# The expert stage of a two-model block: low halves on GpSimd during top-k, wide one-hots, and gate groups spread from the end of top-k

## Chip, cores and metric

The kernel runs on 1 core of one Trainium2 chip. The metric is the device time of one execution in microseconds (us); the time before is the median of 3 runs.

## What is computed

The reference is one first block (state-space mixer, sliding-window attention, gates, and an expert mixer) and two further layers, on 256 tokens of 1024 features in float32. The change lies in the expert mixer, which retrieves 16 of 16384 single-neuron experts in each of 8 heads for every token:

```python
q = (xt @ w_query).reshape(t, PEER_HEADS, 2, PEER_KEY_DIM // 2)
s = jnp.einsum('thkd,hknd->thkn', q, sub_keys)
vals, idx = lax.top_k(s, PEER_TOPK)
cand = (vals[:, :, 0, :, None] + vals[:, :, 1, None, :]).reshape(t, PEER_HEADS, 256)
best, pos = lax.top_k(cand, PEER_TOPK)
expert = i1 * N_SUB_KEYS + i2
gate = softmax(best)
a = einsum('cd,ced->ce', xb, u_tab[eb])
w = gb * gelu(a)
out = einsum('ce,ced->cd', w, v_tab[eb])
```

The kernel does not gather. It computes gelu(x u^T) for all 16384 experts, multiplies by a gate matrix that is zero outside the chosen experts, and multiplies by all of v.

## The kernel before

**Weights as a stream.** `Stream` (lines 80 to 146) loads weight pieces of 128 x 1024 float32 (512 KB) through the queue of SyncE into 3 raw buffers. Each piece is split in two float32r parts: ScalarE casts a high part (`whi`, L125), and VectorE or GpSimd subtracts it from the raw piece to give the low part (`wlo`, L127). A piece is split in two halves of 128 x 512 (`CUT = 2`), and a string names the engine of each half: `'vg'` is the first half on VectorE (v), the second on GpSimd (g); a single letter takes both. There are 3 pairs of part buffers, so the split runs at most 3 pieces ahead of TensorE.

**The product with u.** `gemm_t` (L214) takes 128 pieces of `peer_u`. A piece is 8 blocks of 128 features against 256 tokens, and each block is three matmuls (L210 to L212: high x high, high x low, low x high), so 24 matmuls a piece. `evict` applies Gelu on ScalarE into `store[:, piece, tokens]` (L990). After each piece `step()` issues background work.

**Background work.** `Background.step(n)` runs n steps of the generator `topk`, whose instructions count for the scheduler 200 later than where they stand (`LATE`). `STEP` gives 9 steps in 8 pieces. For each of two halves of the tokens, `topk` computes the scores with 16 float32 matmuls of 64 rows (L1063; two passes each in the trace), finds for each of 8 heads the best 16 of 128 on both sides (`top16`, L1049 to L1053, on VectorE), adds the two lists on GpSimd (L1071), finds the best 16 of 256 sums, then looks up the indices in 16-bit operations (L1076 to L1090) and transposes indices and gates (L1101 to L1105).

**Gate groups.** From piece 80 (`FIRST`) on, `quad(q)` handles 4 tokens. `onehots` makes one-hot columns: A and B by comparison (L957, L958), B times the high part of the gate (L959) on VectorE, B times its low part (L960) on GpSimd. Eight matmuls (L972, L973) form the gates of all 16384 experts for the 4 tokens in one of two PSUM banks. VectorE multiplies the pieces already in `store` by them (L977), ScalarE writes the rest as they are (L979), and later pieces are multiplied as they are evicted (L987 on ScalarE, L988 on VectorE). 64 groups are spread to piece 127. All queues are in order: ScalarE runs L979 after L977, and its later casts wait behind it.

**The product with v** follows (`gemm_acc`, L272 to L274): 128 pieces of 12 matmuls of 512 columns, its left side split from `store` (L1015, L1016).

Of the kernel before, what the change touches and what calls it, by code (L numbers as in the profile page):

```python
# [7 lines left out]
F32 = mybir.dt.float32  # L8
# [71 lines left out]
class Stream:  # L80
    """Weights in the order of their use: loads run ahead, each piece is split into
    two float32r parts whose sum is the float32 value, or is used as it is (lo None)."""
# [12 lines left out]
    def _loads(self, most=None):  # L95
        """A slot is free again when its piece is split, or used where it is not split."""
# [82 lines left out]
class Banks:  # L179
    """PSUM tiles of a bank each, in the given banks in turn."""  # L180
# [10 lines left out]
class Once:  # L191
    """A function called once for each argument."""
# [10 lines left out]
class Kernel:  # L203
# [10 lines left out]
    def gemm_t(self, n_sub, kt, xh, xl, evict, m_per=None, pool=None, step=None):  # L214
        """out^T: per piece of the stream m_per blocks of 128 outputs, tokens along the columns."""
# [76 lines left out]
    def tokens(self):  # L292
        """The two parts of 1024 features of all tokens, the tokens along the columns."""
# [13 lines left out]
    def rsqrt(self, w, y, x):  # L307
        """Newton's iteration, from halved exponent bits."""
# [9 lines left out]
    def residual(self, b, i, ps, sums=True, scale=None):  # L318
        """h += product; the sum of its squares over each half of the row, as 1 / 1024 of it."""
# [14 lines left out]
    def transposed_parts(self, src, i, xh, xl, tp, rev=None):  # L334
        """src: [128 tokens, n]; xh + xl = its transpose, in [128, n / 128, tokens of half i]; rev: a permutation of the tokens."""
# [1342 lines left out]
```

## Time and profile before

| what | value |
|---|---|
| runs | 1868.23, 1873.42, 1876.27 us; median 1873.42 |
| profiled execution | span 1866.1 us, 30817 instructions; no other time is given for it, so its span stands for it, 7.3 us under the median |
| product with u | 355.9 to 857.9 us of the span |
| product with v | from 860.9 us |

Times in the profile are counted from the start of the span. The row of an engine gives its busy time; a matmul's duration overlaps that of the next, so TensorE's pace is read from the distances of starts. "PEclk" is the granted clock as a share of full speed. A wait is put down to what ended it.

### The profile page before, as it was taken

What the parts mean: (1) busy time and instruction counts of PE and PEld (TensorE: products, weight loads), DVE (VectorE), ACT (ScalarE), POOL (GpSimd) and SP (SyncE); (2) the same over time, 40 slices, a digit from 0 to 9 for tenths busy, and PEclk for the clock granted to TensorE, in tenths of its full rate; (3) what the DMA queues carried; (4) which work ended last, traced back from release to release, by engine and by line L of the source; (5) the groups of instructions that cost most, each with busy time, mean ns of one, the idle gap of its engine ahead of it and who ended that gap; (6) DMA issues with size and microseconds to landing.
All of it is one profiled execution on the core that took longest, in us unless ns stands there. A gap on an engine that the chain in (4) does not pass through costs nothing.

```text
span 1866.1 us, 30817 instructions
## 1 busy us (share of the span) xinstructions
PE 1747.6 (94%) x10940; PEld 1532.0 (82%) x10940; DVE 1188.4 (64%) x2521; ACT 899.4 (48%) x2087; POOL 871.3 (47%) x692
## 2 busy tenths in 40 slices
PE   7878899998989988889999999989999998999998
PEld 5456697988989988888888888777799877779986
DVE  7789845377792699996555555567765236775522
ACT  4232544434444433334555555555566445556643
POOL 2465338435444566654444444441354454145443
PEclk9888999989999999999999999999999999999999
DMA  7121235535456533334666666553365555335564
GB/s 251 53 84 46 82 122 171 156 106 168 141 154 182 158 113 102 114 102 159 192 194 195 196 195 192 176 177 105 113 190 183 190 177 185 111 105 192 181 196 143
DMA packets 81543, 282.38 MB, mean 151 GB/s; under 512 B 9659, under 2 KB 12524, under 8 KB 81388
## 3 DMA queue, kind: packets, MB, share of 16 engines
q1 hardware_dynamic: 81388, 280.41, 47.6%
q8 instruction: 86, 1.41, 0.3%
q14 instruction: 69, 0.57, 0.1%
HBM read 279.30 MB, written 1.07 MB: 150 GB/s over the span
## 4 chain that ended last, share of the span: by engine, by line
PE 67%; DVE 19%; issue 5%; POOL 4%; ACT 2%; DMA 2%; SPq 0%; DVEq 0%; POOLq 0%; ACTq 0%
PE acc L272 9%; PE acc L274 9%; PE acc L273 9%; PE acc L210 9%; PE acc L212 9%; PE acc L211 9%; DVE wlo L127 4%; POOL wlo L127 2%; DVE store L988 2%; PE acc L242 1%; PE acc L241 1%; PE acc L243 1%; DVE spare L958 1%; PE o L1396 1%; DVE store L977 1%
## 5 line engine op out<-in xcount | busy, mean ns | idle before, releaser
L127 POOL TENSOR_TENSOR wlo<-raw,whi 128x512 fp32r<-128x512 f32 (+1 forms) x486 | 655.4, 1358 | 700.1 <-ACT whi L125 625.3
L125 ACT CAST whi<-raw 128x512 fp32r<-128x512 f32 (+2 forms) x1004 | 581.8, 612 | 428.3 <-PE acc L211 132.5
L127 DVE TENSOR_TENSOR wlo<-raw,whi 128x512 fp32r<-128x512 f32 (+2 forms) x518 | 437.4, 860 | 320.3 <-ACT whi L125 309.7
L212 PE MATMUL acc<-xh,wlo 128*128 128x256 f32 x1824 | 527.9, 290 | 15.8 <-DVE wlo L127 13.1
L210 PE MATMUL acc<-xh,whi 128*128 128x256 f32 x1824 | 532.6, 293 | 3.1 <-ACT whi L125 2.4
L211 PE MATMUL acc<-xl,whi 128*128 128x256 f32 x1824 | 527.1, 289 | 0.4 <-DVE xl L332 0.3
L212 PEld LDWEIGHTS acc<-xh,wlo 128*128 128x128 f32 x1824 | 358.8, 197 | 21.2 <-DVE wlo L127 16.0
L210 PEld LDWEIGHTS acc<-xh,whi 128*128 128x128 f32 x1824 | 360.2, 198 | 10.0 <-issue 3.6
L211 PEld LDWEIGHTS acc<-xl,whi 128*128 128x128 f32 x1824 | 359.7, 197 | 4.5 <-issue 2.6
L272 PE MATMUL acc<-whi,wh 128*128 128x512 f32 x512 | 199.3, 389 | 2.7 <-ACT wh L1015 2.7
L273 PE MATMUL acc<-wlo,wh 128*128 128x512 f32 x512 | 199.3, 389 | 0.0
L274 PE MATMUL acc<-whi,wl 128*128 128x512 f32 x512 | 199.1, 389 | 0.0
L1015 ACT CAST wh<-store 128x256 fp32r<-128x256 f32 x128 | 51.9, 407 | 160.2 <-PE acc L273 159.3
L1016 DVE TENSOR_TENSOR wl<-store,wh 128x256 fp32r<-128x256 f32 x128 | 54.2, 425 | 114.4 <-ACT wh L1015 114.4
L272 PEld LDWEIGHTS acc<-whi,wh 128*128 128x128 f32 x512 | 96.1, 188 | 23.0 <-ACT wh L1015 3.0
L274 PEld LDWEIGHTS acc<-whi,wl 128*128 128x128 f32 x512 | 96.1, 188 | 19.9
L273 PEld LDWEIGHTS acc<-wlo,wh 128*128 128x128 f32 x512 | 96.1, 188 | 19.8
L273 PE MATMUL acc<-wlo,fh 128*128 128x512 f32 x256 | 99.7, 389 | 0.0
L274 PE MATMUL acc<-whi,fl 128*128 128x512 f32 x256 | 99.7, 389 | 0.0
L272 PE MATMUL acc<-whi,fh 128*128 128x512 f32 x256 | 99.6, 389 | 0.0
L960 POOL TENSOR_TENSOR spare<-spare,gl 128x512 f16<-128x512 f16 x64 | 75.8, 1189 | 49.5 <-PE g L973 38.2
L972 PE MATMUL g<-oh 128*128 128x128 f16 x256 | 63.4, 295 | 21.8 <-ACT store L979 20.9
(382 smaller groups left out, 2656.6 us busy)
## 6 DMA issues: line engine op xcount, KB each, us to landing
raw<-in_peer_u_dram SPq DMA_DIRECT2D x128, 512.0 KB, 3.6
raw<-in_peer_v_dram SPq DMA_DIRECT2D x128, 512.0 KB, 3.6
raw<-in_w_ff_dram SPq DMA_DIRECT2D x128, 512.0 KB, 3.9
raw<-in_w_out_dram SPq DMA_DIRECT2D x24, 512.0 KB, 3.7
raw<-in_w_in_g_dram SPq DMA_DIRECT2D x16, 512.0 KB, 3.7
raw<-in_w_in_qkv_dram SPq DMA_DIRECT2D x12, 512.0 KB, 4.7
raw<-in_w_attn_branch_dram SPq DMA_DIRECT2D x8, 512.0 KB, 3.6
raw<-in_peer_w_query_dram SPq DMA_DIRECT2D x8, 512.0 KB, 4.2
```

What stands on the lines that cost most here:

```text
L125: nc.scalar.copy(hi[:, x], src[:, x])
L127: eng.tensor_tensor(out=lo[:, x], in0=src[:, x], in1=hi[:, x].bitcast(F32), op=OP.subtract)
L210: t.matmul(ps, wh, xh, start=first, stop=False)
L211: t.matmul(ps, wh, xl, start=False, stop=False)
L212: t.matmul(ps, wl, xh, start=False, stop=last)
L272: t.matmul(ps[i][n], xh[:, ts], w[0][:, ns], start=first, stop=False)
L273: t.matmul(ps[i][n], xh[:, ts], w[1][:, ns], start=False, stop=False)
L274: t.matmul(ps[i][n], xl[:, ts], w[0][:, ns], start=False, stop=last)
L960: g.tensor_tensor(out=Bl, in0=B, in1=b(ids[3]), op=OP.mult)
L972: te.matmul(ps[:, t], A[:, :, t], Bh[:, :, t], start=True, stop=False)
L1015: s.copy(wh, store[:, c])
L1016: v.tensor_tensor(out=wl, in0=store[:, c], in1=wh.bitcast(F32), op=OP.subtract)
```

## The change

Six things change in the expert stage; comments elsewhere are dropped and line numbers move by 3 or 4 in `topk`.

```diff
-FIRST = 80
-STEP = lambda c: 1 + (c % 8 == 0)
-PU = 'vg vg gv'
-PU1 = 'vg'
-NU1 = 0
+STEP = lambda c: 1 + c % 2
+PU = 'v'
+PU1 = 'g g gv'
+NU1 = 48
+LAST = 126
...
-                self.acc, tp, gp = self.banks(0, 1, 2), self.banks(7, 6), self.banks(3, 4)
+                self.acc, tp, gp = self.banks(0, 1, 2), self.banks(7, 6), self.banks(3, 4, 5)
...
-                    A, Bh, B, Bl = oh[:, 0], oh[:, 1], spare[:, q % 2], spare[:, 2 + q % 2]
-                    v.tensor_tensor(out=A, in0=io4, in1=b(ids[0]), op=OP.is_equal)
-                    v.tensor_tensor(out=B, in0=io4, in1=b(ids[1]), op=OP.is_equal)
-                    v.tensor_tensor(out=Bh, in0=B, in1=b(ids[2]), op=OP.mult)
-                    g.tensor_tensor(out=Bl, in0=B, in1=b(ids[3]), op=OP.mult)
+                    v.tensor_tensor(out=AB, in0=io4.unsqueeze(1).to_broadcast(both), in1=b(ids), op=OP.is_equal)
+                    v.tensor_tensor(out=B, in0=AB[:, 1].unsqueeze(1).to_broadcast(both), in1=b(gts), op=OP.mult)
...
-                    if c >= FIRST - 6:
-                        self.bg.drain()
-                    want = (T // 4 * (c - FIRST)) // (127 - FIRST)
+                    if done["from"] is None:
+                        if not self.bg.q:
+                            done["from"] = c
+                        return
+                    want = (T // 4 * (c - done["from"])) // (LAST - done["from"])
...
+                ps = [tp.tile([128, 4, 128], F32, name="tp", tag="tp") for _ in range(2)]
+                for x in range(4):
+                    h = 4 * hg + x
+                    for k in range(2):
+                        rows = slice(64 * k, 64 * k + 64)
+                        te.matmul(ps[k][:, x], qT[rows, h, ts], sk[rows, h], start=True, stop=True)
                 for k in range(2):
-                    ps = tp.tile([128, 4, 128], F32, name="tp", tag="tp")
-                    rows = slice(64 * k, 64 * k + 64)
-                    for x in range(4):
-                        h = 4 * hg + x
-                        te.matmul(ps[:, x], qT[rows, h, ts], sk[rows, h], start=True, stop=True)
-                    s.copy(sc[:, k, 4 * hg:4 * hg + 4], ps)
+                    s.copy(sc[:, k, 4 * hg:4 * hg + 4], ps[k])
...
-            v.tensor_copy(ids[0][:, ts], ps[:, 0])
-            v.tensor_copy(ids[1][:, ts], ps[:, 1])
+            v.tensor_copy(ids[:, :, ts], ps[:, 0:2])
```

In words: of the first 48 pieces of u, five of six low halves go to GpSimd; of the other 80, all go to VectorE. `topk` gets 3 steps in 2 pieces. Four one-hot operations of 128 x 512 become two of 128 x 1024, all on VectorE. The gate groups start when `topk` has been issued and end at piece 126. They get a third PSUM bank. The score matmuls alternate between the upper and the lower 64 rows, into two banks.

**How the rows move, 1: GpSimd, first heads of top-k** (L1071, now L1075, is the addition of the two lists of one head; `wlo` rows are low halves, and the numbers tell pieces apart). Before, and then after:

```order
L127 TENSOR_TENSOR wlo_3410<-raw_3297,whi_3409 128x512
L1071 TENSOR_TENSOR store_2822<-store_2822 128x256
L127 TENSOR_TENSOR wlo_3449<-raw_3336,whi_3448 128x512
L1071 TENSOR_TENSOR store_2822<-store_2822 128x256
L127 TENSOR_TENSOR wlo_3494<-raw_3376,whi_3493 128x512
L127 TENSOR_TENSOR wlo_3533<-raw_3415,whi_3532 128x512
L1071 TENSOR_TENSOR store_2822<-store_2822 128x256
```

```order
L127 TENSOR_TENSOR wlo_3424<-raw_3306,whi_3423 128x512
L1075 TENSOR_TENSOR store_2822<-store_2822 128x256
L127 TENSOR_TENSOR wlo_3469<-raw_3345,whi_3468 128x512 x2
L1075 TENSOR_TENSOR store_2822<-store_2822 128x256
L127 TENSOR_TENSOR wlo_3508<-raw_3390,whi_3507 128x512 x2
L1075 TENSOR_TENSOR store_2822<-store_2822 128x256
L127 TENSOR_TENSOR wlo_3553<-raw_3429,whi_3552 128x512
L127 TENSOR_TENSOR wlo_3592<-raw_3474,whi_3591 128x512
```

Between the first and the eighth addition stood 10 low halves of 10 pieces; now there are 15 halves of 9 pieces.

**2: VectorE, in the middle of the gate groups** (L977, now L978, multiplies `store` by a group's gates; L957 to L959, now L960 and L961, make one-hots; L988, now L989, multiplies an evicted piece). Before, and then after:

```order
L977 SCALAR_TENSOR_TENSOR store_2822<-g_7635,store_2822 128x104x4
L957 TENSOR_TENSOR oh_7752<-io4_2872,i1_3154 128x512
L958 TENSOR_TENSOR spare_3158<-io4_2872,i2_3155 128x512
L959 TENSOR_TENSOR oh_7752<-spare_3158,gh_3156 128x512
L957 TENSOR_TENSOR oh_7805<-io4_2872,i1_3154 128x512
L988 TENSOR_TENSOR store_2822<-gt_7679,store_2822 128x128
L977 SCALAR_TENSOR_TENSOR store_2822<-g_7688,store_2822 128x105x4
L977 SCALAR_TENSOR_TENSOR store_2822<-g_7704,store_2822 128x105x4
L127 TENSOR_TENSOR wlo_7716<-raw_7530,whi_7715 128x512
```

```order
L978 SCALAR_TENSOR_TENSOR store_2822<-g_7001,store_2822 128x86x4
L127 TENSOR_TENSOR wlo_7013<-raw_6879,whi_7012 128x512
L961 TENSOR_TENSOR spare_3156<-oh_7049,gts_3155 128x1024
L960 TENSOR_TENSOR oh_7188<-io4_2872,ids_3154 128x1024
L127 TENSOR_TENSOR wlo_7064<-raw_6916,whi_7063 128x512
L989 TENSOR_TENSOR store_2822<-gt_7045,store_2822 128x128
L978 SCALAR_TENSOR_TENSOR store_2822<-g_7052,store_2822 128x87x4
```

The period between two gate multiplications now holds both low halves of a piece and one wide operation of each kind. The first L978 stands at 47 pieces.

**3: TensorE, the scores of the first tokens** (L1063, now L1066; the other rows are the product with u). Before, and then after:

```order
L210 MATMUL acc_3417<-xh_2826,whi_3330 128x256
L1063 MATMUL tp_3194<-store_2822 128x128
L211 MATMUL acc_3417<-xl_2827,whi_3330 128x256
L1063 MATMUL tp_3194<-store_2822 128x128
L212 MATMUL acc_3417<-xh_2826,wlo_3331 128x256
L1063 MATMUL tp_3194<-store_2822 128x128
```

```order
L211 MATMUL acc_3392<-xl_2827,whi_3300 128x256
L1066 MATMUL tp_3192<-store_2822 128x128
L212 MATMUL acc_3392<-xh_2826,wlo_3301 128x256
L1066 MATMUL tp_3193<-store_2822 128x128
L1066 MATMUL tp_3192<-store_2822 128x128
L1066 MATMUL tp_3193<-store_2822 128x128
```

Each score matmul stood between two matmuls of the product; now 7 of the first 8 stand in a row, and the two banks alternate. The 32 score matmuls stand in 4 bunches, two per half of the tokens, with one or two matmuls of the product inside each.

## Rows read from the trace of the kernel before

**Rows 1.** The page: busy time, share of the span and instructions of each engine.

```profile
PE 1747.6 (94%) x10940; PEld 1532.0 (82%) x10940; DVE 1188.4 (64%) x2521; ACT 899.4 (48%) x2087; POOL 871.3 (47%) x692
```

**Rows 2.** Stretches: length; busy (instructions) PE, PEld, DVE, ACT, POOL; PEclk, DMA, GB/s.

```profile
373.20:397.40 24.20, 24.20 (x107) 19.26 (x106) 13.09 (x66) 6.58 (x13) 5.17 (x6) 0.72 0.22 70
...
423.40:450.10 26.70, 21.79 (x170) 20.46 (x169) 25.25 (x51) 12.54 (x25) 11.48 (x8) 1.00 0.45 137
...
476.00:501.90 25.90, 25.90 (x157) 21.89 (x156) 20.82 (x78) 9.41 (x19) 10.00 (x9) 0.93 0.33 106
...
530.80:558.80 28.00, 22.85 (x170) 21.88 (x170) 24.41 (x40) 12.95 (x25) 12.66 (x9) 0.94 0.49 154
558.80:628.20 69.40, 69.40 (x581) 69.40 (x581) 20.42 (x28) 33.95 (x72) 31.92 (x25) 1.00 0.60 184
628.20:857.90 229.70, 207.94 (x1666) 202.37 (x1664) 221.85 (x338) 83.03 (x254) 142.85 (x111) 0.97 0.37 112
857.90:860.90 3.00, 0.25 (x3) 0.06 (x1) 1.91 (x3) 1.92 (x5) 1.26 (x1) 1.00 0.81 261
```

**Rows 3.** Timeline of ScalarE, 595 to 612 us: two evictions (start, duration).

```profile
597.17 0.38 ACT L990 ACTIVATE store<-acc 128x256 f32<-128x256 f32 x1
...
600.05 0.38 ACT L990 ACTIVATE store<-acc 128x256 f32<-128x256 f32 x1
```

**Rows 4.** Waits, 628.2 to 857.9 us (total us, times, longest).

```profile
ACT store L979 <- DVE store L977: 124.1, 57, 4.5
...
PE g L972 <- ACT store L979: 20.9, 20, 2.5
```

**Rows 5.** Waits, 373 to 560 us (total us, times, longest).

```profile
POOL store L1071 <- DVE store L1052: 28.8, 12, 7.0
...
PE acc L212 <- DVE wlo L127: 9.8, 8, 2.5
```

**Rows 6.** Timeline of TensorE, 845.9 to 846.6 us: matmuls of one gate group.

```profile
845.61 0.30 PE L973 MATMUL g<-spare,oh 128*128 128x128 f16 x1
...
846.32 0.29 PE L973 MATMUL g<-spare,oh 128*128 128x128 f16 x1
```

**Rows 7.** Timeline of TensorE, 379 to 394 us: score matmuls, two passes each.

```profile
385.78 0.49 PE L1063 MATMUL tp<-store 64*128 64x128 f32 x2
...
386.51 0.48 PE L1063 MATMUL tp<-store 64*128 64x128 f32 x2
...
388.86 0.79 PE L1063 MATMUL tp<-store 64*128 64x128 f32 x2
...
390.09 0.79 PE L1063 MATMUL tp<-store 64*128 64x128 f32 x2
```

**Rows 8.** Line L127, 566 to 628 us (ns min/median/max, first and last start).

```profile
L127 POOL TENSOR_TENSOR wlo<-raw,whi x22: 1291/1292/1301, 566.2 to 627.0; 128x512 fp32r<-128x512 f32 x22
L127 DVE TENSOR_TENSOR wlo<-raw,whi x21: 691/693/1040, 568.2 to 626.1; 128x512 fp32r<-128x512 f32 x21
```

**Rows 9.** Lines L957, L977, L988 (ns min/median/max), 632 to 858 us.

```profile
L957 DVE TENSOR_TENSOR oh<-io,i x60: 407/411/1525, 632.2 to 849.6; 128x512 f16<-128x512 f16 x60
...
L977 DVE SCALAR_TENSOR_TENSOR store<-g,store x64: 481/578/680, 633.4 to 855.5; 128x332 f32<-128x332 f32 x2, 128x344 f32<-128x344 f32 x2, 128x356 f32<-128x356 f32 x2, 128x368 f32<-128x368 f32 x2
...
L988 DVE TENSOR_TENSOR store<-gt,store x46: 160/1131/1454, 636.3 to 854.6; 128x4 f32<-128x4 f32 x1, 128x8 f32<-128x8 f32 x1, 128x16 f32<-128x16 f32 x1, 128x20 f32<-128x20 f32 x1
```

**Rows 10.** VectorE in top-k, 400 to 570 us: groups by shape; line L1089; the page's L1016.

```profile
L1052 DVE MAX8 store<-store 128x8 f32<-128x128 f32 x25 | 6.7, 273 | 0.0
...
L1049 DVE MAX8 store<-store 128x8 f32<-128x256 f32 x14 | 5.9, 422 | 1.1 <-POOL store L1071 0.8
...
L1053 DVE MATCH_VALUE_LOAD store<-store 128x8 f32 x40 | 2.9, 72 | 0.1
...
L1089 DVE TENSOR_TENSOR store<-store x12: 277/686/1772, 436.2 to 551.9; 128x1024 f16<-128x1024 f16 x4, 128x512 f16<-128x512 f16 x4, 128x256 f16<-128x256 f16 x4
...
L1016 DVE TENSOR_TENSOR wl<-store,wh 128x256 fp32r<-128x256 f32 x128 | 54.2, 425 | 114.4 <-ACT wh L1015 114.4
```

More of the change, by code (lines that the diff above doesn't have):

```diff
@@ L944, in peer @@
                 self.gemm_t(8, 8, xh, xl, lambda m, ps: s.copy(qT[:, m], ps))
-                ids = [w.tile([128, T], F16, name=n) for n in ("i1", "i2", "gh", "gl")]
-                self.bg.add(self.topk(w, tp, scratch, qT, sk, iota, ids))
-                done = {"t": 0, "c": 0, "q": 0, "oh": {}}
-                spare = self.const.tile([128, 4, 128, 4], F16, name="spare", tag="gain")
-                def onehots(q):
-                    ts = slice(4 * q, 4 * q + 4)
-                    b = lambda x: x[:, ts].unsqueeze(1).to_broadcast([128, 128, 4])
-                    oh = self.stay.tile([128, 2, 128, 4], F16, name="oh", tag="xr", bufs=XR)
-                    A, Bh, B, Bl = oh[:, 0], oh[:, 1], spare[:, q % 2], spare[:, 2 + q % 2]
-                    v.tensor_tensor(out=A, in0=io4, in1=b(ids[0]), op=OP.is_equal)
-                    v.tensor_tensor(out=B, in0=io4, in1=b(ids[1]), op=OP.is_equal)
-                    v.tensor_tensor(out=Bh, in0=B, in1=b(ids[2]), op=OP.mult)
-                    g.tensor_tensor(out=Bl, in0=B, in1=b(ids[3]), op=OP.mult)
-                    done["oh"][q] = (A, Bh, Bl)
+                ids = w.tile([128, 2, T], F16, name="ids")
+                gts = w.tile([128, 2, T], F16, name="gts")
+                self.bg.add(self.topk(w, tp, scratch, qT, sk, iota, ids, gts))
+                done = {"t": 0, "c": 0, "q": 0, "oh": {}, "from": None}
+                spare = self.const.tile([128, 2, 2, 128, 4], F16, name="spare", tag="gain")
+                both = [128, 2, 128, 4]
+                def onehots(q):
+                    b = lambda x: x[:, :, 4 * q:4 * q + 4].unsqueeze(2).to_broadcast(both)
+                    AB = self.stay.tile(both, F16, name="oh", tag="xr", bufs=XR)
+                    B = spare[:, q % 2]
+                    v.tensor_tensor(out=AB, in0=io4.unsqueeze(1).to_broadcast(both), in1=b(ids), op=OP.is_equal)
+                    v.tensor_tensor(out=B, in0=AB[:, 1].unsqueeze(1).to_broadcast(both), in1=b(gts), op=OP.mult)
+                    done["oh"][q] = AB[:, 0], B[:, 0], B[:, 1]
                 def quad(q):
@@ L1027, in peer, with topk @@
                 self.gemm_acc(range(128), Once(lhs), ps, self.residual)
-    def topk(self, w, tp, scratch, qT, sk, iota, ids):
+    def topk(self, w, tp, scratch, qT, sk, iota, ids, gts):
         nc = self.nc
@@ L1101, in topk @@
                 te.transpose(ps[:, k], e3[:, k], self.ident)
-            v.tensor_copy(ids[0][:, ts], ps[:, 0])
-            v.tensor_copy(ids[1][:, ts], ps[:, 1])
-            v.tensor_scalar(ids[2][:, ts], ps[:, 2], 1024.0, None, op0=OP.mult)
-            v.scalar_tensor_tensor(ids[3][:, ts], ps[:, 2], 1024.0, ids[2][:, ts], op0=OP.mult, op1=OP.subtract)
+            v.tensor_copy(ids[:, :, ts], ps[:, 0:2])
+            v.tensor_scalar(gts[:, 0, ts], ps[:, 2], 1024.0, None, op0=OP.mult)
+            v.scalar_tensor_tensor(gts[:, 1, ts], ps[:, 2], 1024.0, gts[:, 0, ts], op0=OP.mult, op1=OP.subtract)
             yield
```

## The prediction, made before the run

> **What bounds the kernel now.** The page comes first: TensorE is busy 94% of the span and VectorE 64% [rows 1], but a mean hides stages, so the second view is the table of stretches over the product with u. Its pace is set by TensorE alone where nothing else happens: two evictions lie 2.88 us apart [rows 3], and 24 pieces (581 matmuls, 24 a piece) take 69.4 us at full clock [rows 2], 2.89 each. The other stretches are read against this floor, with the pieces counted by dividing the matmuls by 24.
>
> Scores: 3 pieces take 24.2 us where 8.6 would do, and 5 take 25.9 where 14.4 would do; together 27.1 us over the floor, at clocks of 0.72 and 0.93 [rows 2]. Rest of top-k: twice 7 pieces (170 matmuls) take 26.7 and 28.0 us where 20.2 would do, 14.3 us over, with VectorE nearly full [rows 2]. There TensorE's third matmul waits for a low part from VectorE [rows 5]. Gate stage: 48 pieces (1666 matmuls less 512 of the groups) take 229.7 us where 138.2 would do, 91.5 over, and VectorE is busy for 221.9 of it [rows 2]. So three quarters of the time lies at the floor, and the last stretch is VectorE's.
>
> Of the 91.5 us, TensorE's own matmuls take some: starts within a group lie (846.32 - 845.61) / 6 = 0.118 us apart [rows 6], 512 x 0.118 = 60.4. The other 31.1 is waiting. The waits name it: ScalarE stood 124.1 us behind VectorE's L977, and TensorE 20.9 us for ScalarE's L979 to free a bank of the gates [rows 4]. Then comes 3.0 us before the product with v starts [rows 2]. The stage in total is 128 x 2.88 = 368.6, plus 60.4, 27.1, 14.3, 31.1, 3.0 and a remainder of 0.5: 505.0 us. The change leaves the first two terms as they are; only 76 us can be won, all of it in the other terms.
>
> **Gate stage: 31.1 us becomes 3.** The groups now start near piece 46 and end at 126, so 80 pieces carry 64 groups, 0.80 each. TensorE then needs 2.88 + 0.80 x 8 x 0.118 = 3.63 us a piece. VectorE's share: a low half takes 0.69 us while nothing holds it up, two are 1.39 [rows 8]. Blocked operations are much longer: the same comparison of 128 x 512 takes 0.41 us at best and 1.53 at worst, and a multiplication of at most 256 columns has a median of 1.13 although one of 256 columns takes 0.43 elsewhere [rows 9, 10]. GpSimd has no work left in this stage, by the order, so I take the short ends. A wide one-hot operation does not exist before; its nearest row is the 16-bit one of 128 x 1024 in L1089, among whose shapes the median 0.686 is that shape's undisturbed time [rows 10], and twice the comparison, 0.82, bounds it above while nothing blocks it [rows 9]. I take 0.69. L978 works on 47 to 126 pieces times 4 columns: from (680 - 481) ns over 508 - 332 columns [rows 9], 1.13 ns a column, I get 0.50 us at the mean of 86 pieces. L989 is 0.16 to 0.43, 0.29 at the mean. The sum is 1.39 + 0.29 + 0.80 x (2 x 0.69 + 0.50) = 3.18 us a piece under TensorE's 3.63. A piece that carries a group needs 3.56 against 3.82, so it fits even singly, though by little. Near the end L978 is 0.68 and L989 0.43, 3.88 against 3.82, and every fifth piece without a group pays that back. The order supports this: after L978 stands the second low half, whose cast is not behind that group's L980, then both one-hot operations, so VectorE rarely waits. The third bank takes the 20.9 us of bank waits off. What is late next is the eviction behind L980. I leave 3 us; the ends are 0 and the present 31.
>
> The four low-gate multiplications on GpSimd vanish into VectorE, counted above. Loads of weights are the same in number and order on SyncE's queue, and at 3.63 us a piece they come slower than now.
>
> **Scores: 27.1 becomes 15.** All 32 score matmuls stood singly. At full clock one plus the matmul it precedes takes 0.73 us, at half clock 1.23 [rows 7]. Now they stand in 4 bunches. A pair of passes lasts 0.48 to 0.49 us at full clock [rows 7]: 32 x 0.48 = 15.4. Below, alternating halves could run side by side, 7.7; above, nothing changes, 27.1. The clock fell to its lower level (1.2 of 2.4 GHz) in these stretches while TensorE ran scores and product in turn; whether bunches avoid that no row shows. I take 15. The Trainium skill, page "TensorEngine Tiling (Array Packing)", section "Key Properties", says that changing the tiling mode drains the engine and that different tiles can compute in parallel. By that the sum would be the lower end, 7 us better than mine. No row here has such a pair, and I keep the serial price.
>
> **Top-k: 14.3 becomes 18.** A head costs VectorE two searches of 128 columns and one of 256: 2 x (5 x 0.273 + 3 x 0.072) + 5 x 0.42 + 3 x 0.072 = 5.5 us [rows 10]. By the order, 7 heads now pass while 9 pieces are split: 38.5 us plus two low halves, 40, against 25.9 on TensorE. Before, 7 heads took 10 pieces: 38.5 + 6.9 = 45 against 28.8. The deficit is 14 instead of 16 per half of the tokens, and 3 part buffers, 8.6 us, cover some of it. In its favour before, score matmuls of the second four heads filled TensorE's time; they now come earlier. So the heads themselves are about even. The lookups after them are the risk: their 16-bit operations take 0.69 or 1.77 us for the same shape [rows 10], a difference of about one GpSimd subtraction, 1.29 [rows 8], and GpSimd now does 1.67 halves a piece instead of one. I add 4 us: 18, with ends of 6 and, in the rival below, 67.
>
> The rule behind these rows is in the Trainium skill, page "SBUF — State Buffer", section "Who interferes with whom": a VectorE instruction with two SBUF inputs and a GpSimd instruction that reads SBUF block one another. The trace agrees for the lookups (0.69 and 1.77), and by it the first 48 pieces are where this change can lose.
>
> **Start of v: 3.0 becomes 1.5**, since the last groups stand at piece 126 with two pieces behind them; ends 0 and 3.
>
> The sum: 368.6 + 60.4 + 15 + 18 + 3 + 1.5 + 0.5 = 467 against 505, which is 38 us less. I allow 3 us for the first group, which stands right behind the second half's lookups on VectorE: 35 us. The profiled execution would go from 1866.1 to 1831; its span is 7.3 us under the median of the runs, so from the median 1873.4 I predict **1838 us**.
>
> **Rivals.**
> - *Everything fits, and pairs of scores overlap.* Scores 8, top-k 8, nothing for the first group: 20 us better, 1818. For it: no engine is full on the new counts. Against: VectorE is full in top-k in either order.
> - *Half of it.* Gate stage left with 15 of its 31 us, since ScalarE still waits behind L978 once a group and a group's period has only 0.26 us of slack on VectorE: 1850 to 1858.
> - *The wide operations run at one element a cycle, or the range of patterns slows them.* Two low halves of 512 float32 columns cost 1.39 [rows 8], so 1024 columns at that pace cost about 1.3. VectorE needs 1.39 + 0.29 + 0.80 x (2.6 + 0.5) = 4.16 a piece, 0.53 over TensorE, 80 x 0.53 = 42 us of waiting, more than the 31 now: the 39 us in its place eat the gain, and the time is 1874 to 1878, no change. Against: the 16-bit rows of 2 and 4 patterns already run faster than that.
> - *Top-k is throttled by GpSimd.* GpSimd waited for VectorE before 12 additions, 28.8 us in all and 7.0 at worst [rows 5]. It then held half of the low parts; now it holds five of six, and each wait delays the next pieces. If the prefetch covers nothing, 14 intervals cost 5.9 (a head and its share of low halves) less 9 / 7 x 2.88 = 3.7, 2.2 each, 31 us, and the 28 two-input operations of the lookups at 1.29 us of blocking each add 36: 67 instead of 18, which makes it 1887, **slower**. It decides against the change from a top-k loss of 18 + 35 = 53 us.
>
> That the change does not do what it says can be set aside for the order: the rows above show the moves.
>
> **How the numbers follow.** The forecast has a chance of 0.50, everything fits 0.14, half of it 0.15, the wide operations 0.09, GpSimd 0.12. About 0.5% of 1873, 9 us, is what a measurement can tell from no change. Faster by more than that: 0.50 + 0.14 + 0.15 less a small share of the worst of these, 0.77; within it 0.11; slower 0.12. The range runs from 1816, the everything-fits case, to 1868, past the half case; it leaves out most of the last two rivals and a little below.
>
> **What would show it.** In the profile after: GpSimd idle from about piece 48 to the end of u; L127 on VectorE near 0.69 us there, L960 and L961 near 0.69 and L989 under 0.45; no wait of TensorE for L980; steps of 3.6 us a piece with VectorE at some 88%. In top-k: score rows in bunches, and waits of TensorE for a low part from GpSimd instead of VectorE. The prediction is wrong if the gate stage runs above 3.8 us a piece, if wide operations cost over 1 us, or if TensorE loses over 50 us in the first 48 pieces.

## The result, and the profile after

| | before | after |
|---|---|---|
| median of the runs (lowest to highest), us | 1870.83 (1866.82 to 1876.27), 4 runs | 1826.06 (1824.68 to 1826.87), 4 runs |
| profiled execution: span, us | 1866.1 | 1822.9 (its time 1824.68) |
| first matmul of u, us of the span | 355.9 | 350.7 |
| from there to the first matmul of v, us | 504.9 | 465.2 |
| the rest, us | 1005.3 | 1007.0 |

The change is **faster**: ratio 0.9771, 95% interval 0.9743 to 0.9799. It is inside the range, 12 us below the predicted 1838. Of the 43.2 us between the two spans, 39.7 lie in the product with u; 5.2 lie ahead of it, in code that the change does not touch (the last section comes back to that), and the rest is 1.7 longer.

The page's first lines of the changed kernel (busy time, share of the span, instructions) answer to [rows 1]. GpSimd has 153 us less to do and VectorE 46 us less, but which stretch that helps these shares don't tell:

```profile
span 1822.9 us, 30616 instructions
...
PE 1722.8 (95%) x10940; PEld 1517.9 (83%) x10940; DVE 1142.4 (63%) x2537; ACT 907.9 (50%) x2120; POOL 718.2 (39%) x580
```

The stretches of the changed kernel answer to [rows 2], columns as there: scores of the first half of the tokens, its last heads and lookups, scores of the second half, its heads and lookups, the gate stage, the start of v.

```profile
368.00:377.70 9.70, 9.70 (x83) 8.82 (x83) 7.92 (x44) 5.06 (x10) 4.47 (x5) 1.00 0.37 126
...
398.00:429.20 31.20, 24.27 (x170) 23.25 (x170) 29.58 (x74) 13.29 (x27) 23.11 (x17) 0.89 0.46 147
...
445.00:456.40 11.40, 11.40 (x96) 10.39 (x96) 11.38 (x37) 5.06 (x10) 5.63 (x5) 1.00 0.45 136
...
466.00:507.60 41.60, 32.31 (x237) 31.00 (x237) 39.10 (x139) 16.69 (x33) 27.98 (x24) 0.88 0.43 140
...
516.20:812.90 296.70, 296.70 (x2483) 293.35 (x2483) 224.42 (x431) 139.99 (x389) 2.39 (x2) 1.00 0.49 149
812.90:815.90 3.00, 0.32 (x3) 0.11 (x1) 1.78 (x2) 1.85 (x5) 1.49 (x2) 1.00 0.52 183
```

The gate stage is read with the floor of the prediction: 2483 matmuls less 512 of the groups are 82.1 pieces, 82.1 x 2.88 + 60.4 = 296.9 us, and the stretch lasts 296.7. TensorE waits for nothing. The scores: 83 matmuls less 32 passes are 2.1 pieces, 6.1 us of 9.7; the other stretch has 2.7 pieces, 7.7 of 11.4. What is left over, 3.6 and 3.7 us, was 15.2 and 10.9 before when the pieces are counted in the same way, and the clock is at full speed where it was at 0.72 and 0.93 [rows 2]. The lookups, 31.2 us for 7.1 pieces (20.4) and 41.6 for 9.9 (28.4), now lose most.

The lines of VectorE in the gate stage (ns min/median/max) answer to [rows 8, 9]:

```profile
L127 DVE TENSOR_TENSOR wlo<-raw,whi x162: 675/691/695, 516.9 to 811.0; 128x512 fp32r<-128x512 f32 x162
...
L960 DVE TENSOR_TENSOR oh<-io,ids x60: 681/685/690, 521.9 to 791.7; 128x1024 f16<-128x1024 f16 x60
...
L961 DVE TENSOR_TENSOR spare<-oh,gts x62: 681/685/689, 521.3 to 801.6; 128x1024 f16<-128x1024 f16 x62
...
L978 DVE SCALAR_TENSOR_TENSOR store<-g,store x64: 346/512/673, 520.4 to 808.7; 128x188 f32<-128x188 f32 x1, 128x192 f32<-128x192 f32 x1, 128x196 f32<-128x196 f32 x1, 128x204 f32<-128x204 f32 x1
...
L989 DVE TENSOR_TENSOR store<-gt,store x80: 154/286/1391, 528.9 to 811.6; 128x12 f32<-128x12 f32 x2, 128x28 f32<-128x28 f32 x2, 128x44 f32<-128x44 f32 x2, 128x60 f32<-128x60 f32 x2
```

Minimum and maximum lie within 20 ns of each other in the first three lines: nothing holds VectorE up. L989's median fell from 1131 to 286 ns; its widths grow from a few columns to 256 in both kernels. VectorE is busy for 224.4 of the 296.7 us, 76%, where the prediction expected some 88%. It had added up durations, which come to 252.5 us here, but a row of VectorE starts about 0.08 us before the row ahead of it ends, where the two stand back to back:

```profile
608.31 0.68 DVE L127 TENSOR_TENSOR wlo<-raw,whi 128x512 fp32r<-128x512 f32 x1
608.91 0.68 DVE L961 TENSOR_TENSOR spare<-oh,gts 128x1024 f16<-128x1024 f16 x1
```

The waits of this stretch (us in total, times, longest) answer to [rows 4]; none is TensorE's, and ScalarE's for L978 is 34.3 us where it was 124.1:

```profile
ACT whi L125 <- PE acc L211: 98.4, 65, 2.4
...
ACT store L980 <- DVE store L978: 34.3, 61, 1.5
```

### The profile page after: what moved, and what is told of

It is laid out like the page before. It is cut to its first block, busy times and chain, and to the rows that moved or that the text cites. A ratio compares the mean times of both kernels' runs of the same rounds, so it can differ in the third digit from the quotient of the medians.

```text
span 1822.9 us, 30616 instructions
## 1 busy us (share of the span) xinstructions
PE 1722.8 (95%) x10940; PEld 1517.9 (83%) x10940; DVE 1142.4 (63%) x2537; ACT 907.9 (50%) x2120; POOL 718.2 (39%) x580
## 4 chain that ended last, share of the span: by engine, by line
PE 73%; DVE 15%; POOL 4%; issue 4%; DMA 2%; ACT 2%; SPq 0%; POOLq 0%; DVEq 0%; ACTq 0%
PE acc L210 10%; PE acc L212 10%; PE acc L211 10%; PE acc L274 9%; PE acc L272 9%; PE acc L273 9%; DVE wlo L127 2%; POOL wlo L127 2%; PE g L973 2%; PE g L974 2%; PE acc L242 1%; PE acc L243 1%; PE acc L241 1%; PE o L1399 1%; PE tp L741 1%
## 5 line engine op out<-in xcount | busy, mean ns | idle before, releaser
L127 POOL TENSOR_TENSOR wlo<-raw,whi 128x512 fp32r<-128x512 f32 (+2 forms) x438 | 581.6, 1341 | 872.6 <-ACT whi L125 821.9
L127 DVE TENSOR_TENSOR wlo<-raw,whi 128x512 fp32r<-128x512 f32 (+1 forms) x566 | 447.8, 805 | 328.9 <-ACT whi L125 312.8
L212 PE MATMUL acc<-xh,wlo 128*128 128x256 f32 x1824 | 523.3, 287 | 20.1 <-DVE wlo L127 10.4
L212 PEld LDWEIGHTS acc<-xh,wlo 128*128 128x128 f32 x1824 | 354.8, 195 | 24.5 <-DVE wlo L127 11.8
L210 PEld LDWEIGHTS acc<-xh,whi 128*128 128x128 f32 x1824 | 356.3, 196 | 10.9 <-ACT whi L125 5.2
L211 PEld LDWEIGHTS acc<-xl,whi 128*128 128x128 f32 x1824 | 356.1, 195 | 3.5 <-issue 2.4
L272 PEld LDWEIGHTS acc<-whi,wh 128*128 128x128 f32 x512 | 96.5, 189 | 22.8 <-ACT wh L1018 2.9
L273 PEld LDWEIGHTS acc<-wlo,wh 128*128 128x128 f32 x512 | 96.4, 188 | 20.1
L242 PE MATMUL acc<-wlo,xh 128*128 128x512 f32 (+2 forms) x176 | 67.8, 385 | 4.5 <-DVE wlo L127 4.5
L241 PE MATMUL acc<-whi,xh 128*128 128x512 f32 (+2 forms) x176 | 66.1, 382 | 2.1 <-ACT xr L395 1.8
```

Source lines behind the costliest of these rows:

```text
L127: eng.tensor_tensor(out=lo[:, x], in0=src[:, x], in1=hi[:, x].bitcast(F32), op=OP.subtract)
L210: t.matmul(ps, wh, xh, start=first, stop=False)
L211: t.matmul(ps, wh, xl, start=False, stop=False)
L212: t.matmul(ps, wl, xh, start=False, stop=last)
L241: t.matmul(o, x1, wh, start=k == 0, stop=False)
L242: t.matmul(o, x1, wl, start=False, stop=False)
```

## The experiments

Each run is split into the terms of the prediction's sum, from the starts of TensorE's pieces in its profiled execution: 2.88 us a piece and 0.118 a gate matmul are the floor (429.0 us), and what a piece takes beyond that belongs to the stretch in which it lies. "Start" is the first matmul of u, "stage" runs from there to the first of v. What is left of the stage is the start of v, 2.9 us (5.5 in e4, whose last group stands behind the last piece); the sums hold within 1 us. Each ratio is against runs of the kernel before on the same chip.

| run | median us | ratio, 95% | start | scores | top-k | gates | stage |
|---|---|---|---|---|---|---|---|
| before | 1870.83 | | 355.9 | 26.0 | 15.8 | 31.1 | 504.9 |
| after | 1826.06 | 0.9771 (0.9743 to 0.9799) | 350.7 | 7.9 | 25.1 | 0.3 | 465.2 |
| e9_before_spread | 1843.46 | 0.985 (0.9821 to 0.9879) | 350.5 | 26.1 | 15.4 | 9.5 | 482.9 |
| e12_before_wide | 1836.92 | 0.9817 (0.9799 to 0.9835) | 351.2 | 26.1 | 15.2 | 0 | 473.1 |
| e3_two_banks | 1831.97 | 0.9793 (0.9757 to 0.983) | 355.8 | 7.9 | 25.3 | 0.2 | 465.3 |
| e4_groups_late | 1832.25 | 0.979 (0.9758 to 0.9823) | 356.7 | 7.8 | 25.5 | 0 | 466.8 |
| e5_onehots_old | 1829.15 | 0.9783 (0.9762 to 0.9805) | 351.2 | 7.9 | 26.3 | 0.3 | 466.5 |
| e6_low_late_shared | 1827.25 | 0.9773 (0.9749 to 0.9797) | 351.8 | 7.9 | 25.2 | 0.3 | 465.3 |
| e10_late_both | 1830.09 | 0.9768 (0.9746 to 0.9789) | 356.1 | 7.9 | 25.5 | 0 | 465.2 |
| e1_scores_runs | 1831.9 | 0.9803 (0.9771 to 0.9835) | 351.2 | 14.4 | 22.8 | 0.1 | 469.2 |
| e2_before_scores | 1876.3 | 1.0037 (1.0021 to 1.0053) | 352.3 | 24.1 | 20.3 | 35.9 | 512.3 |
| e8_slow98 | 1843.6 | 0.9853 (0.983 to 0.9876) | 353.5 | 28.8 | 22.2 | 0.3 | 483.3 |
| e7_low_early_shared | 1823.74 | 0.9753 (0.9728 to 0.9779) | 351.7 | 8.0 | 20.1 | 0.4 | 460.4 |
| e11_paced | 1828.18 | 0.9759 (0.974 to 0.9777) | 360.7 | 5.8 | 21.8 | 0.3 | 459.8 |

The stage is the better measure of a part: the start differs by up to 6 us among runs whose code ahead of it is the same (all but e11), more than most parts are worth.

### Gate stage: which part takes the 31 us away

**One part of the change undone at a time.** e3, two gate banks again:

```diff
-self.banks(3, 4, 5)
+self.banks(3, 4)
```

> The changed kernel with two PSUM banks for the gates instead of three. Theory: the 20.9 us of bank waits before came from VectorE being full and groups coming 1.36 a piece; with 0.8 groups a piece and VectorE at 76% two banks are enough: 1825 to 1829. Rival: the third bank carries a good part of the gain: 1838 to 1846.

e4, gate groups from piece 80 on:

```diff
-if not self.bg.q:
+if not self.bg.q and c >= 80:
```

> The changed kernel with the 64 gate groups held back to pieces 80 to 126, as before, and all else as changed. Theory (what counted is GpSimd's absence, which takes VectorE's operations to their short times; the spread adds slack): VectorE needs 1.39 + 0.29 + 1.39 x 1.95 = 4.39 us a piece there, TensorE 2.88 + 1.39 x 0.944 = 4.19, so some 10 us come back, 15 with bursts of two groups: 1834 to 1842. Rival (the spread is the main cause): all 31 us of the gate stage come back, 1855 or more.

e5, four narrow one-hot operations as before, one of them on GpSimd:

```diff
...
-v.tensor_tensor(out=AB, in0=io4.unsqueeze(1).to_broadcast(both), in1=b(ids), op=OP.is_equal)
-v.tensor_tensor(out=B, in0=AB[:, 1].unsqueeze(1).to_broadcast(both), in1=b(gts), op=OP.mult)
+v.tensor_tensor(out=A, in0=io4, in1=b(ids[:, 0]), op=OP.is_equal)
+v.tensor_tensor(out=B, in0=io4, in1=b(ids[:, 1]), op=OP.is_equal)
+v.tensor_tensor(out=Bh, in0=B, in1=b(gts[:, 0]), op=OP.mult)
+g.tensor_tensor(out=Bl, in0=B, in1=b(gts[:, 1]), op=OP.mult)
```

> The changed kernel with the four one-hot operations of 128 x 512 as before, the low-gate multiplication on GpSimd (0.8 of 1.19 us a piece). Theory (GpSimd and VectorE block one another when both read SBUF twice or at all): each of them holds up one of VectorE's two-input operations by up to 1.2 us, VectorE goes from 3.18 to about 3.9 us a piece against TensorE's 3.63, and 15 to 25 us come back: 1841 to 1851. Rival (only the count of VectorE's work matters, which falls by 0.11 us a piece): 1824 to 1828.

e6, the late low halves shared with GpSimd again:

```diff
-PU = 'v'
+PU = 'vg vg gv'
```

> The changed kernel with one low half of each piece from 48 on given back to GpSimd. Theory (blocking): VectorE loses 0.69 us of work a piece and gains about 1.0 of blocking by a 1.29 us operation, 3.5 against 3.63; within 10 us of the changed kernel, 1826 to 1836, with VectorE's operations long in the trace. Rival (blocking costs the full 1.29 or more a piece, three operations held up): 1850 or more.

Measured: none costs the stage more than 1.6 us. e3 and e4 are some 6 us above the changed kernel in their medians, but their start is 5 and 6 us later and their stage is not. In e5 GpSimd's multiplication is back, and L989 shows its blocking, 1102 ns in the median. In e6, where GpSimd has low halves alone, L989 is at 307 ns, but there L961 is held up, 1597 ns in the median where it takes 685 with GpSimd idle:

```profile
L989 DVE TENSOR_TENSOR store<-gt,store x66: 198/1102/1247, 562.6 to 798.0; 128x44 f32<-128x44 f32 x2, 128x60 f32<-128x60 f32 x2, 128x72 f32<-128x72 f32 x2, 128x88 f32<-128x88 f32 x2
```

```profile
L989 DVE TENSOR_TENSOR store<-gt,store x66: 189/307/1327, 562.1 to 798.7; 128x44 f32<-128x44 f32 x2, 128x60 f32<-128x60 f32 x2, 128x72 f32<-128x72 f32 x2, 128x88 f32<-128x88 f32 x2
...
L961 DVE TENSOR_TENSOR spare<-oh,gts x52: 1215/1597/1767, 562.5 to 797.2; 128x1024 f16<-128x1024 f16 x52
```

From 560 to 800 us these rows of L989 add up to 61.7 us in e5 and those of L961 to 80.7 in e6; in the changed kernel the two lines take 19.5 and 35.6 there. So the blocking is real in both, 42 and 45 us, and there is room for it: in these 240 us VectorE is busy for 221.3 us in e5 and 195.2 in e6. The theories of e4 and e5, 10 to 25 us back, failed: they added up VectorE's durations as the prediction did, and counted more of its time than is busy. No part undone alone brings the stall back; either none matters, or several suffice. Two undone at once, and one part put alone into the kernel before, tell these apart.

**Two undone at once.** e10 has e4's and e6's edits together, that is, groups from piece 80 with shared low halves, as before.

```diff
-PU = 'v'
+PU = 'vg vg gv'
...
-if not self.bg.q:
+if not self.bg.q and c >= 80:
```

> The changed kernel without two of its edits at once: groups held back to pieces 80 to 126, and one low half of each piece from 48 on on GpSimd. Theory: VectorE's work is 0.69 + 0.29 + 1.39 x 1.95 = 3.7 us a piece, and one GpSimd operation of 1.29 us a piece blocks it for 0.5 to 1.0 more, 4.2 to 4.7 against TensorE's 4.19: the gate stage loses 5 to 20 us, the product with u takes 472 to 487 us instead of 465. Rival (VectorE's own work decides, blocking does not): nothing is lost, 465 to 468.

Measured: the gates still lose nothing, and the theory, 5 to 20 us lost, failed. The stretch of groups in e10 stays at TensorE's pace (1427 matmuls with no idle time, 170.00 us) while VectorE is busy for 97% of it. In the kernel before (second row) VectorE is busy for 98.8% of a stretch amid the groups, and TensorE idles for 21.8 us of it:

```profile
640.00:810.00 170.00, 170.00 (x1427) 167.72 (x1426) 165.28 (x251) 73.40 (x219) 56.07 (x41) 1.00 0.42 128
```

```profile
650.00:840.00 190.00, 168.24 (x1334) 163.21 (x1334) 187.72 (x288) 65.70 (x205) 117.79 (x91) 0.96 0.36 109
```

**One part alone in the kernel before.** e9 starts the groups at the end of top-k; e12 has the two wide one-hot operations, both on VectorE, and nothing else. The edits, against the kernel before:

```diff
...
-if c >= FIRST - 6:
-    self.bg.drain()
-want = (T // 4 * (c - FIRST)) // (127 - FIRST)
+if done["from"] is None:
+    if not self.bg.q:
+        done["from"] = c
+    return
+want = (T // 4 * (c - done["from"])) // (127 - done["from"])
```

> The kernel before with the spread alone: groups from the end of top-k (piece 62) to 127, 0.97 a piece instead of 1.36; GpSimd keeps one low half of each piece and the low-gate multiplication. Theory (VectorE's time with its blocking against TensorE's decides; the spread and GpSimd's absence each give enough slack only beside the other edits): low half 1.0, eviction 0.95, 0.97 x 2.5 for the group, all at the blocked means of before, is 4.4 us a piece against TensorE's 2.88 + 0.97 x 0.944 = 3.80, so most of the waiting stays, 1860 to 1875. Rival (slack by the spread alone is enough): the 31 us of the gate stage go, 1836 to 1844.

```diff
...
-v.tensor_tensor(out=A, in0=io4, in1=b(ids[0]), op=OP.is_equal)
-v.tensor_tensor(out=B, in0=io4, in1=b(ids[1]), op=OP.is_equal)
-v.tensor_tensor(out=Bh, in0=B, in1=b(ids[2]), op=OP.mult)
-g.tensor_tensor(out=Bl, in0=B, in1=b(ids[3]), op=OP.mult)
+v.tensor_tensor(out=AB, in0=io4.unsqueeze(1).to_broadcast(both), in1=b(ids), op=OP.is_equal)
+v.tensor_tensor(out=B, in0=AB[:, 1].unsqueeze(1).to_broadcast(both), in1=b(gts), op=OP.mult)
...
```

> The kernel before with the two wide one-hot operations alone, all four parts on VectorE: groups still from piece 80 to 127, one low half of each piece still on GpSimd, two banks. Theory after the runs so far (GpSimd's one-hot operation, 64 times in 47 pieces, is what blocks VectorE; without it there is enough room even without the spread): the 31 us of the gate stage fall to 0 to 5, the product with u takes 474 to 482 us instead of 505 and the run 1838 to 1848. Rival (the third bank, or the low halves on VectorE, is needed beside it): 12 to 25 us of waiting stay, 1850 to 1865.

Measured: the spread takes 21.6 of the 31.1 us, which is more than the theory of e9 allowed (1860 to 1875 us, and 1843.5 came); the wide operations take all of it. The stretch, L989 and L961, and the wait for the gate multiplication of e12:

```profile
625.00:830.00 205.00, 202.31 (x1666) 198.43 (x1665) 188.80 (x286) 88.94 (x260) 66.05 (x49) 0.99 0.44 131
```

```profile
L989 DVE TENSOR_TENSOR store<-gt,store x47: 158/305/1468, 631.0 to 822.4; 128x4 f32<-128x4 f32 x1, 128x8 f32<-128x8 f32 x1, 128x16 f32<-128x16 f32 x1, 128x20 f32<-128x20 f32 x1
```

```profile
L961 DVE TENSOR_TENSOR spare<-oh,gts 128x1024 f16<-128x1024 f16 x62 | 71.9, 1160 | 6.6 <-PE g L974 6.6
```

```profile
ACT store L980 <- DVE store L978: 68.0, 64, 2.1
```

This stretch holds 1136 matmuls of u, the 512 of the groups and 18 of v. At the floor, u and the groups take 136.3 + 60.4 = 196.7 us of TensorE in it, and VectorE is busy for 188.8 us, where the gate stage before had 221.9 [rows 2]. TensorE's only idle time is the 2.7 us ahead of v. The durations of the one-hot operations add up to 111.5 us where the three on VectorE took 117.4 before, and L961 is still held up by low halves. L989 went from 42.0 us (as L988) to 21.8 and the low halves from 47.6 to 35.8, so most of what VectorE gained lies in lines that no edit of e12 touches.

In e9 the groups have more time, but VectorE is busy for 98.6% of a stretch amid them, the wait behind L977 is as long as before [rows 4], and TensorE still waits for L979 to free a bank:

```profile
590.00:800.00 210.00, 206.24 (x1701) 202.43 (x1700) 207.11 (x310) 87.25 (x263) 136.58 (x104) 1.00 0.44 134
```

```profile
ACT store L979 <- DVE store L977: 124.5, 53, 5.2
...
PE g L972 <- ACT store L979: 4.1, 14, 0.7
```

What follows: 31 us of stall had two cures that don't add up. In the kernel before, the wide operations are enough; the spread gives two thirds of it; beside the wide operations the third bank and VectorE's low halves are not needed. The kernels whose gates stall are those whose VectorE is hardly ever free amid the groups, busy for 98.8% before, 98.9% in e2 and 98.6% in e9; at 97% (e10) nothing is lost. A kernel with the four narrow operations all on VectorE was not tried. That the gain of e12 lies in other lines than the one-hot operations speaks for GpSimd's leaving rather than the width, but which of the two does it is not shown.

### Scores: alternation, bunching, or both

e1 keeps the bunches and takes the halves one after the other; e2 puts the alternating score matmuls alone into the kernel before; e8 keeps alternation in the changed kernel and gives top-k its old pace.

```diff
-for x in range(4):
-    h = 4 * hg + x
-    for k in range(2):
-        rows = slice(64 * k, 64 * k + 64)
+for k in range(2):
+    rows = slice(64 * k, 64 * k + 64)
+    for x in range(4):
+        h = 4 * hg + x
```

> The changed kernel with the score matmuls in runs of four on the same 64 rows, no longer alternating between the upper and the lower rows; their place and bunching stay much as they are. Theory: it is the alternation that saves time, since passes on the two halves of the rows run side by side (14 passes took 1.16 us, 0.083 each). Then each bunched matmul goes back to about 0.43 us and the few that stand singly to 0.6: the scores cost about 19 us over the floor instead of 8, and the time is 1834 to 1840. Rival: it is the bunching that saves, and alternation does nothing: 1826 to 1830.

```diff
-    ps = tp.tile([128, 4, 128], F32, name="tp", tag="tp")
-    rows = slice(64 * k, 64 * k + 64)
-    for x in range(4):
-        h = 4 * hg + x
-        te.matmul(ps[:, x], qT[rows, h, ts], sk[rows, h], start=True, stop=True)
+ps = [tp.tile([128, 4, 128], F32, name="tp", tag="tp") for _ in range(2)]
+for x in range(4):
+    h = 4 * hg + x
+    for k in range(2):
+        rows = slice(64 * k, 64 * k + 64)
+        te.matmul(ps[k][:, x], qT[rows, h, ts], sk[rows, h], start=True, stop=True)
```

> The kernel before with the alternating score matmuls alone; each still stands singly between matmuls of the product. Theory (side by side needs neighbours): no gain, 1867 to 1873. Rival (alternation alone is enough, wherever they stand): 19 us less, about 1852.

```diff
-STEP = lambda c: 1 + c % 2
+STEP = lambda c: 1 + (c % 8 == 0)
...
-NU1 = 48
+NU1 = 62
```

> The changed kernel with top-k spread as before, 9 steps in 8 pieces, GpSimd taking the low halves of the first 62 pieces, groups from about piece 61. The scores then stand singly again. Theory: that gives back most of what the scores gained, 15 to 19 us, and the slower top-k loses about 10 us less than the 24.8 of the changed kernel; the gate stage still fits (VectorE 1.39 + 0.29 + 0.97 x 1.9 = 3.5 under TensorE's 3.8): 1830 to 1838. Rival: the pace of top-k does not matter for the scores, and the time is 1815 to 1820.

Measured: 7.9 us with both, 14.4 with bunches that don't alternate (the theory had 19, the rival 8), 24.1 and 28.8 where alternating matmuls stand singly. e8 takes 1843.6 us, more than both its theory and its rival. TensorE's timeline (start, duration; x counts passes) of the changed kernel, then of e1, then of e2:

```profile
367.94 0.48 PE L1066 MATMUL tp<-store 64*128 64x128 f32 x2
...
368.68 1.16 PE L1066 MATMUL tp<-store 64*128 64x128 f32 x14
...
370.43 1.29 PE L1066 MATMUL tp<-store 64*128 64x128 f32 x12
```

```profile
368.49 0.48 PE L1066 MATMUL tp<-store 64*128 64x128 f32 x2
...
369.22 1.49 PE L1066 MATMUL tp<-store 64*128 64x128 f32 x14
```

```profile
370.16 0.49 PE L1063 MATMUL tp<-store 64*128 64x128 f32 x2
...
370.89 0.49 PE L1063 MATMUL tp<-store 64*128 64x128 f32 x2
```

A single pair and its neighbour take 0.73 us in e2 as before [rows 7]; 14 passes side by side take 1.16, in runs of four 1.49. The edit of e1 also made the bunches finer: the 32 passes of its first stretch stand as 2, 14, 6, 4, 2, 2 and 2, with alternation as 2, 14, 12 and 4. And the clock fell in this stretch of e1, to 0.74 (1.2 and 2.4 GHz are its two levels, 0.50 and 1.00), while it stayed at 1.00 in the second:

```profile
368.00:381.00 13.00, 13.00 (x70) 11.05 (x69) 8.27 (x46) 5.20 (x10) 3.68 (x4) 0.74 0.37 110
...
451.00:464.00 13.00, 13.00 (x90) 10.99 (x89) 12.98 (x51) 5.51 (x11) 6.46 (x5) 1.00 0.32 105
```

Over the floor its first scores cost 8.0 us and its second 6.4, where the changed kernel has 3.9 and 4.0. The bunches are made by the pace: two steps of top-k are issued behind one piece. In e8, whose scores stand singly again, the clock is down as well, at 0.69, where the changed kernel's rows above have 1.00:

```profile
373.00:395.00 22.00, 22.00 (x94) 17.73 (x95) 12.20 (x70) 5.16 (x10) 6.56 (x7) 0.69 0.23 68
```

TensorE is busy for all 22.00 us of it. What follows: bunches alone are worth 11.6 us (26.0 to 14.4), alternation another 6.5 once there are bunches, with what the finer bunches and the lower clock of e1 cost. By the stretch at full clock it is 2.4 us in each half of the tokens, 4.8. Alone it gives 1.9 us of the scores, and e2 is 0.4% slower than the kernel before, with 4.5 and 4.8 us more in the top-k and gate terms; how the alternation leads to these was not looked into further.

### Top-k: GpSimd's share and the pace

e7 gives GpSimd half of the early low halves instead of five of six; e11 does so too, at one step a piece, with the score matmuls issued at the front of the scheduler's order.

```diff
-PU1 = 'g g gv'
+PU1 = 'vg vg gv'
```

> The changed kernel with the first 48 pieces split as before, one half on each engine. Theory: VectorE gets 0.69 instead of 0.23 us a piece while top-k fills it, 45 x 0.46 = 21 us, of which some comes back as GpSimd blocks the lookups less: 5 to 15 us longer, 1831 to 1841. Rival (the loss in the lookups, most of the 24.8 us of top-k, comes from GpSimd's five of six halves): 5 to 10 us shorter, 1816 to 1821.

```diff
-STEP = lambda c: 1 + c % 2
+STEP = lambda c: 1
...
-PU1 = 'g g gv'
-NU1 = 48
+PU1 = 'vg vg gv'
+NU1 = 69
...
-te.matmul(ps[k][:, x], qT[rows, h, ts], sk[rows, h], start=True, stop=True)
+with self.tc.high_priority():
+    te.matmul(ps[k][:, x], qT[rows, h, ts], sk[rows, h], start=True, stop=True)
```

> A version meant to beat the changed one: top-k at one step a piece, its low halves shared as before ('vg vg gv' for the first 69 pieces, then all on VectorE), and the score matmuls taken out of the background, so that they stand in neighbouring pairs or bunches whatever the pace. Theory: scores cost 8 to 12 us over the floor, top-k 8 to 15 instead of 25 (a head of 5.5 us and 3 low halves of 0.69 now has 3 pieces, 8.6 us), the gate stage still fits with 1.08 groups a piece (3.8 against 3.9): the product with u takes 448 to 458 us instead of 465 and the run 1809 to 1820. Rival (top-k's loss is in the lookups, which block each other with GpSimd at any pace): top-k stays at 20 to 25, 465 us, 1824 to 1830.

Measured: with the halves shared, top-k loses 20.1 us instead of 25.1, so the five of six cost 5 us; the theory of e7, 5 to 15 us longer, failed, and its rival came close. TensorE's waits in top-k of the changed kernel, and the row of e7 from the last product ahead of u to the end of top-k:

```profile
PE acc L212 <- DVE wlo L127: 7.2, 2, 4.3
PE acc L212 <- POOL wlo L127: 7.1, 7, 1.6
```

```profile
350.00:516.00 166.00, 151.51 (x1219) 145.21 (x1218) 141.07 (x484) 77.83 (x157) 77.94 (x63) 1.00 0.51 150
```

TensorE idles for 16.2 us in the two stretches of lookups of the changed kernel, for 10.1 in those before [rows 2] and for 14.5 in all of e7's row. So 1.7 of the 5 us are waiting. Beside the rest stands the clock, 0.89 and 0.88 in these two stretches against 1.00 in e7; TensorE stood idle for up to 4.3 us at a time in the changed kernel, for 1.8 at most in e7. By these shares the lower clock costs at most 3.4 + 5.0 us, an estimate from 0.11 of 31.2 and 0.12 of 41.6; no run shows it by itself. The other 4.3 over the kernel before are not separated: e2, with the old pace and the old share, has 20.3 as well, e8, with the old pace and five of six, 22.2. What GpSimd does to the lookups is seen in VectorE's timeline of the changed kernel, and in GpSimd's beside it (five low halves back to back):

```profile
413.41 1.56 DVE L1093 TENSOR_TENSOR store<-store 128x1024 f16<-128x1024 f16 x1
...
415.01 1.39 DVE L1093 TENSOR_TENSOR store<-store 128x512 f16<-128x512 f16 x1
...
417.60 1.37 DVE L1093 TENSOR_TENSOR store<-store 128x256 f16<-128x256 f16 x1
```

```profile
412.68 7.45 POOL L127 TENSOR_TENSOR wlo<-raw,whi 128x512 fp32r<-128x512 f32 x5 [3.25 <-ACT whi L125]
```

While they run, an operation on 256 columns takes as long as one on 512, about one GpSimd subtraction [rows 8]. e7 has the best median, 1823.74 us, but its interval overlaps that of the changed kernel: that it beats it is shown by the stage (4.8 us), not by the times. e11 has the shortest stage, 459.8 us, but part of its scores moved ahead of the product with u, which starts at 360.7, 4 us later than in any other run here; nothing is won over e7, and its time of 1828.2 us missed the forecast of 1809 to 1820. e7's halves with other paces were not tried.

## Why the prediction was right

- **The floor** (368.6 and 60.4): held; the gate stretch is within 0.2 us of it.
- **Gates, 31.1 to 3**: measured 0.3. The durations were right: wide operations 0.685 us (forecast 0.69), low half 0.691, L978 0.512 (0.50), L989 0.286 (0.29). "Half of it" and "the wide operations run at one element a cycle" both fell on these rows. The test, VectorE's time against TensorE's, holds in the runs: the gates stall where VectorE is hardly ever free (98.8% before, 98.6% in e9) and not at 97% (e10). But the sum was too high, some 88% where 76% came, since it added up durations that overlap; the error lay on the safe side. And the reason was too wide: it summed all the edits, and e12 shows one of them to be enough. The 31.1 us were called waiting; TensorE's idle time is 21.8 of them [rows 2], and the granted clock of 0.97 there, 1.00 after, stands beside the rest.
- **Scores, 27.1 to 15**: mis-sized, measured 7.9 (26.0 before, by starts of pieces). I took 0.48 us for each matmul in a bunch because no row had two halves side by side, and put the overlap at the lower end, 7.7. The runs show that end, 14 passes in 1.16 us. The prediction named the Trainium skill, page "TensorEngine Tiling (Array Packing)", section "Key Properties", for it: both of its sentences agree with the runs, tiles in parallel (1.16 against 1.49 us) and a cost of changing between tilings (0.73 us for a single pair and its neighbour). With 14.4 against 7.9, e1 shows what taking it at its word was worth: 6.5 us, of which 4.8 by the stretch at full clock.
- **Top-k, 14.3 to 18**: mis-sized the other way, measured 25.1 (15.8 before, by starts of pieces). The direction and the place (lookups beside GpSimd's subtractions) were right, but of what I put at 4 us, GpSimd's share alone is 5 by e7, with the lower clock in it, and 4 more are not accounted for. The sign that TensorE would wait for low parts from GpSimd instead of VectorE came by half: 7.1 us for GpSimd, 7.2 for VectorE. The slower rival would have needed 67. GpSimd's 12 waits for VectorE were 20.1 us in place of 28.8 [rows 5]: they did not grow.
- **Start of v, 3.0 to 1.5**: wrong, 2.9. I had the last groups in mind, but the last evictions count. The timeline of the changed kernel there:

```profile
813.88 1.26 POOL L127 TENSOR_TENSOR wlo<-raw,whi 128x512 fp32r<-128x512 f32 x1 [0.75 <-ACT whi L125]
814.12 1.30 DVE L989 TENSOR_TENSOR store<-gt,store 128x256 f32<-128x256 f32 x1 [2.13 <-ACT gt L988]
...
815.45 1.02 ACT L1018 CAST wh<-store 128x256 fp32r<-128x256 f32 x3 [0.86 <-DVE store L989]
...
815.91 0.50 PE L272 MATMUL acc<-whi,wh 128*128 128x512 f32 x1 [2.69 <-ACT wh L1018]
```

  L989 comes just after GpSimd's first low half of v and takes 1.30 us, where an operation of that shape takes 0.43 [rows 10].
- **First group, 3 us**: nothing of it is seen.

The sum was 470 us with the first group, and 465.2 came: 7 us too much for scores, 3 for gates, 3 for the first group, against 7 too little in top-k and 1.4 at v. That the errors of scores and top-k cancel is luck. Some 7 us of the 12 between the predicted and the measured time lie outside the stage: its start was 5.2 us earlier, and I carried over the 7.3 us by which the median stood above the profiled span, which is 3.2 after; the rest is 1.7 longer.

## What to carry to other kernels

Read an engine's share where the work stands, and read the stretch against its floor: VectorE at 97% cost nothing (e10), while 98.6% went with 9.5 us lost (e9). Taken from 550 to 820 us, which has pieces without groups, e9 would show 93%, less than e10. An engine's durations added up can exceed its busy time. Undo a change's parts in pairs before giving each a share. Matmuls of part of the rows pay off when they stand together and alternate between the halves, so look at the order that the scheduler makes of them, not at the loop. Beside GpSimd's long subtractions, two-input operations of VectorE are the expensive place, and the short ones most for their size.

## What the runs showed of the hardware that was not expected

- **The clock fell on a busy TensorE.** In e8 and in the kernel before it was 0.69 and 0.72 in the score stretch, with TensorE busy in all of it, and in the first stretch of e1, whose bunches don't alternate, 0.74; alternating bunches of the same number kept 1.00. That the many changes between 64 and 128 rows cause it was not tried by itself.
- **GpSimd's two kinds of work held up different lines of VectorE.** The Trainium skill, page "SBUF — State Buffer", section "Who interferes with whom", says that a VectorE instruction with two SBUF inputs contends with a GpSimd instruction that reads SBUF, and the runs agree: L989 takes 286 ns in the median with GpSimd idle and 1102 with its one-hot multiplication back; with low halves alone it takes 307, and L961 1597 instead of 685. L978, which reads the gates from PSUM, is not held up: 527 ns on average in the changed kernel, 519 in e5 and 522 in e6, all from 560 to 800 us. So one line's median does not show how much an engine is held up in all.
- **Code that no edit touches starts u at 350.5 to 356.7 us.** Near the beginning of the span the clock was lower in the kernel before than after (its stretch first, then that of the changed kernel):

```profile
58.00:76.00 18.00, 14.30 (x36) 7.33 (x37) 15.79 (x34) 2.90 (x6) 9.16 (x3) 0.54 0.26 71
```

```profile
56.00:72.00 16.00, 12.94 (x42) 6.86 (x43) 15.56 (x34) 2.62 (x5) 6.63 (x3) 0.69 0.22 66
```

  These few us are not the change's. The clock there does not settle them: from 56 to 76 us it is 0.74 in e4, which starts u at 356.7, and 0.75 in the changed kernel, which starts it at 350.7. What sets them stays open.
